# Splitting weights into a rounded and a rest part: casts by ScalarE and VectorE, or two DMAs of GpSimd

## The chip, the cores and the metric

The kernel runs on one core of a Trainium2 chip. A core has TensorE (PE: matrix products), VectorE (DVE), ScalarE (ACT) and GpSimd (POOL) for elementwise work, SyncE (SP) that here only issues DMAs, and 16 DMA engines between the chip's memory (HBM) and the core's own (SBUF). PE writes its results into eight banks of PSUM. Each engine works through a queue of its own, in order; an instruction whose inputs are not there yet holds up all that stand behind it in the same queue.

The metric is the time of the whole program on the device in microseconds (us), median of several runs.

## The reference, cut to what matters

Four layers of mixed kinds work on 1040 tokens (16 learned ones and 1024 of the input) with 1024 channels: attention over a sliding window, mLSTM, HGRN2, and attention again. Each layer normalizes its input, multiplies it by a large matrix, mixes over time, and multiplies by an output matrix:

```
for i in range(DEPTH):
    kind = i % N_MIXERS
    u = rmsnorm(h, norm_gain[i])
    if kind == 0:   y = attention_branch(u, a_w_in[j], ..., a_w_out[j], valid, pos)
    elif kind == 1: y = mlstm_branch(u, b_w_in[j], ..., b_w_out[j], valid)
    else:           y = hgrn2_branch(u, c_w_in[j], ..., c_w_out[j], valid)
    h = h + jnp.where(valid[None, :, None], y, 0.0)
```

All of it is float32. The change concerns the two products `u @ w_in` and `y @ w_out` alone, and in them only how the weights come into SBUF.

## The kernel before

**Products in two parts.** PE's faster format fp32r keeps fewer bits than float32. So the kernel splits each operand: `h` is the operand rounded to fp32r, `l` is what the rounding left (operand minus `h`, rounded in turn), and a product becomes three: h·h, h·l and l·h. The activations are split once into `uh` and `ul`; the weights are split tile by tile as they are loaded.

**Weight tiles.** A tile is 128 x 1024 numbers (512 KB), laid out by the host so that each of 128 partitions reads 4 KB in one run. There are 176 of them: 28 in each attention layer, 80 in the mLSTM layer, 40 in the HGRN2 layer. `proj` (line 242, matmuls on line 259) uses one tile for 128 output channels over three chunks of tokens (400, 384 and 256 columns), 72 matmuls per tile. `proj_v` (line 276, matmuls on lines 300 and 304) uses two tiles at a time, the two halves of the contraction, alternately for each block of 128 tokens. `proj_out` (line 320, matmuls on line 349) also holds two tiles, one for each half of the output channels.

**How a tile gets in.** `weights` (line 229) takes a buffer for `h` and one for `l` from two rings, tags `wh` and `wl`, of three buffers each. It works in two halves of 512 columns: SP loads the raw half into a ring of two buffers (`wr`, line 237); ScalarE rounds it into `h` (line 192); VectorE subtracts and writes `l` (line 193). Four pairs of tiles (`inrow=True`, one pair near the end of each layer) use buffers of the ring of rows, `r`, instead of `wh` and `wl`. One small matrix of the mLSTM layer goes through `gate_weights` (line 195), which takes a `wh` buffer for both of its parts.

**Order of the work.** The order of PE's instructions is written out by hand: `steps` is a list of (estimated PE time, function, preparation). The last loop of `hybrid_kernel` (line 1363) walks it and calls each tile's preparation, which is `weights`, as soon as the summed estimates between the step at hand and the tile's first use are below `LOOKAHEAD` (12000 ns). On the other engines a scheduler orders the instructions ahead of time from estimated durations; what was written earlier has priority. Buffers of a ring are handed out in turn, so a tile's `l` waits until PE has used the `l` three tiles earlier for the last time.

**What else is on POOL.** In the attention layers POOL writes the sink column of each score tile (line 630) and scales the exponentials by the reciprocal of their sum (line 638); PE's transposes of the result (line 650) wait for that. In the HGRN2 layer it copies small diagonal blocks (line 1169), in the mLSTM layer it sets a column of ones in each value tile (line 856). It issues no DMA.

Of the kernel before, what the change touches and what calls it, by code (L numbers as in the profile page):

```python
# [9 lines left out]
F32 = mybir.dt.float32  # L10
F32R = mybir.dt.float32r
AF = mybir.ActivationFunctionType
ALU = mybir.AluOpType
PSUM = bass.MemoryType.PSUM

P = 128
D = 1024
KT = D // P
# [13 lines left out]


B_COLS = 96
LOOKAHEAD = 12000.0
TAIL_LAG = 600.0
PRIO = 40
ROWS, TMPS, RAWS, YS = 8, 6, 2, 3
XS = 14
GAP, BURST = 200.0, 1300.0  # L40
KT_LAG, ATT_LAG = 900.0, 600.0
# [68 lines left out]
def hybrid_kernel(ctx: ExitStack, tc: tile.TileContext, ins, out, layers=(0, 1, 2, 3)):  # L110
    nc = tc.nc
    v, s, g, pe, sp = nc.vector, nc.scalar, nc.gpsimd, nc.tensor, nc.sync
# [3 lines left out]
    wpool = ctx.enter_context(tc.tile_pool(name="wpool", bufs=1))  # L116
# [7 lines left out]
    def nm(x):  # L124
        ctr[0] += 1
        return f"{x}{ctr[0]}"

    def row():
        return rpool.tile([P, T], F32, tag="r", name=nm("r"), bufs=ROWS)

    def rrow():
        return rpool.tile([P, T], F32R, tag="r", name=nm("r"), bufs=ROWS)
# [58 lines left out]
    def split(src, h, l):  # L191
        s.copy(h, src)  # L192
        v.tensor_tensor(l, src, h.bitcast(F32), op=ALU.subtract)  # L193

    def gate_weights(src):

        w = wpool.tile([P, 1024], F32R, tag="wh", name=nm("wh"), bufs=3).rearrange("p (k z c) -> p k z c", k=KT, z=2)
        raw = row()[:, :512]
        sp.dma_start(raw, src)
        raw = raw.rearrange("p (k c) -> p k c", k=KT)  # L200
        split(raw, w[:, :, 0], w[:, :, 1])
        return w

    def gate_rows_proj(src, evac):

        st = {}

        def pre():
            st["w"] = gate_weights(src)

        groups = []
        for n, (c0, cn) in enumerate(CHUNKS):
            grp = []
            for part in range(4):
                def fn(n=n, c0=c0, cn=cn, part=part):
                    if part == 0:
                        st[n] = psj()
                    for k in (2 * part, 2 * part + 1):
                        for i, b in enumerate((uh, ul)):
                            pe.matmul(st[n][:, :cn], st["w"][:, k].rearrange("p z c -> p (z c)"), b[:, k, c0 : c0 + cn],  # L220
                                      start=(k == 0 and i == 0), stop=(k == KT - 1 and i == 1))
                    if part == 3:
                        evac(st[n], n, c0, cn)

                grp.append([4 * cn * MM, fn, pre if (n == 0 and part == 0) else None])
            groups.append(grp)
        return groups

    def weights(src, kind, inrow=False):
        if inrow:  # L230
            h, l = (rrow()[:, :1024] for _ in range(2))
        else:
            h = wpool.tile([P, 1024], F32R, tag="wh", name=nm("wh"), bufs=3)
            l = wpool.tile([P, 1024], F32R, tag="wl", name=nm("wl"), bufs=3)
        for z in (slice(0, 512), slice(512, 1024)):
            raw = wpool.tile([P, 512], F32, tag="raw", name=nm("wr"), bufs=RAWS)
            sp.dma_start(raw, src[:, z])
            split(raw, h[:, z], l[:, z])
        k = dict(m=8, v=4, o=2)[kind]
        return h.rearrange("p (k c) -> p k c", k=k), l.rearrange("p (k c) -> p k c", k=k)  # L240

    def proj(src, evac, chunks=CHUNKS):
        st = {}

        def pre():
            st["w"] = weights(src, "m")

        groups = []
        for n, (c0, cn) in enumerate(chunks):
            grp = []  # L250
            for part in range(4):
                def fn(n=n, c0=c0, cn=cn, part=part):
                    if part == 0:
                        st[n] = psj()
                    h, l = st["w"]
                    acc = st[n]
                    for k in (2 * part, 2 * part + 1):
                        for i, (a, b) in enumerate(((h, uh), (h, ul), (l, uh))):
                            pe.matmul(acc[:, :cn], a[:, k, :], b[:, k, c0 : c0 + cn],  # L259
                                      start=(k == 0 and i == 0), stop=(k == KT - 1 and i == 2))  # L260
                    if part == 3:
                        evac(acc, n, c0, cn)

                grp.append([6 * cn * MM, fn, pre if (n == 0 and part == 0) else None])
            groups.append(grp)
        return groups
# [9 lines left out]
    def proj_v(src0, src1, evac):  # L276
        st = {}

        def pre0():
            st[0] = weights(src0, "v")  # L280

        def pre1():
            st[1] = weights(src1, "v")
# [1071 lines left out]
    ahead, k = 0.0, 0  # L1355
# [6 lines left out]
    k = 0  # L1362
    for n, (cost, fn, pre) in enumerate(steps):
        while k < len(steps) and (k <= n or ahead < LOOKAHEAD):
            if steps[k][2]:
# [119 lines left out]
```

## Time and profile before

| | us |
|---|---|
| three runs, median (lowest to highest) | 2641.04 (2640.87 to 2641.67) |
| the profiled execution | 2644.26 |
| its span, first to last instruction | 2642.5 |

The stretches of the span belong to: attention 0 to about 495, mLSTM to about 1590, HGRN2 to about 2190, attention again to the end. A row of the costliest groups names the line, the engine, the operation, the tile written and the tiles read, shape and count, then busy time in all and the mean of one, and at last the idle time of the engine just ahead of these instructions with what ended it. A matmul's duration in the trace is longer than the distance to the next one, since matmuls overlap in the pipeline; the distance is what it costs.

### The profile page before, as it was taken

How to read it: one execution, taken by the hardware profiler on the slowest of the kernel's cores; microseconds unless marked ns; L12 is line 12 of the kernel's file. 1: busy time of each engine (PE TensorE's matmuls, PEld its weight loads, DVE VectorE, ACT ScalarE, POOL GpSimd, SP SyncE). 2: the span in 40 equal slices, each digit the busy share in tenths (PEclk: the TensorE clock that was granted, in tenths of full speed). 3: DMA queues.
4: the chain of work that ended last, by engine and by line, in shares of the span. 5: the costliest groups of instructions: out<-in, count | busy, mean ns of one | idle time of the engine just before them, and what ended most of it. 6: DMA issues, size and time to landing. Idle time of an engine off the chain costs nothing.

```text
span 2642.5 us, 54003 instructions
## 1 busy us (share of the span) xinstructions
PE 2577.0 (98%) x20276; PEld 2476.4 (94%) x20276; DVE 1969.1 (75%) x5324; ACT 1688.6 (64%) x4339; POOL 247.2 (9%) x502
## 2 busy tenths in 40 slices
PE   7999999999999999999999999999999999999999
PEld 5899989999999999999999999999999998999999
DVE  6887797974747474746465688979887979887896
ACT  7777767555454545454545657878685857767773
POOL 2221221000000000000000000100000000321330
PEclk9999999999999999999999999999999999999999
DMA  4213111011111111111111101011110113212112
GB/s 129 67 50 91 47 44 43 26 61 56 41 57 41 57 41 57 41 57 41 53 45 49 49 26 50 30 38 34 34 42 30 38 50 91 59 42 83 55 37 80
DMA packets 82438, 136.10 MB, mean 52 GB/s; under 512 B 12016, under 2 KB 34928, under 8 KB 82176
## 3 DMA queue, kind: packets, MB, share of 16 engines
q1 hardware_dynamic: 82176, 132.65, 15.9%
q8 instruction: 160, 2.62, 0.4%
q14 instruction: 102, 0.84, 0.1%
HBM read 117.76 MB, written 4.26 MB: 46 GB/s over the span
## 4 chain that ended last, share of the span: by engine, by line
PE 74%; DVE 12%; ACT 8%; DMA 2%; issue 2%; SPq 1%; POOL 0%; DVEq 0%; ACTq 0%; POOLq 0%
PE pj L259 35%; PE pj L349 15%; PE pj L304 10%; PE po L669 1%; ACT Sm L635 1%; PE pt L650 1%; PE po L894 1%; PE pa L908 1%; PE po L896 1%; DVE wl L193 1%; DVE Sm L632 1%; SPq L523 1%; PE pm L1141 1%; PE pj L300 1%; ACT wh L192 1%
## 5 line engine op out<-in xcount | busy, mean ns | idle before, releaser
L259 PE MATMUL pj<-uh,wh 128*128 128x256 f32 (+2 forms) x2688 | 925.9, 344 | 9.6 <-ACT uh L192 9.4
L259 PE MATMUL pj<-ul,wh 128*128 128x256 f32 (+2 forms) x2688 | 867.1, 323 | 3.0 <-DVE ul L193 2.5
L259 PE MATMUL pj<-uh,wl 128*128 128x256 f32 (+2 forms) x2688 | 863.8, 321 | 0.0
L259 PEld LDWEIGHTS pj<-uh,wh 128*128 128x128 f32 x2688 | 509.4, 189 | 31.3 <-ACT uh L192 13.5
L259 PEld LDWEIGHTS pj<-ul,wh 128*128 128x128 f32 x2688 | 509.9, 190 | 16.3 <-DVE ul L193 6.7
L259 PEld LDWEIGHTS pj<-uh,wl 128*128 128x128 f32 x2688 | 509.3, 189 | 0.0
L192 ACT CAST wh<-wr 128x512 fp32r<-128x512 f32 x336 | 201.9, 615 | 99.1 <-PE pj L349 31.4
L193 DVE TENSOR_TENSOR wl<-wr,wh 128x512 fp32r<-128x512 f32 x336 | 232.3, 700 | 42.7 <-ACT wh L192 40.7
L349 PE MATMUL pj<-yh,wh 128*128 128x384 f32 (+2 forms) x768 | 253.1, 330 | 9.9 <-DVE x L352 6.7
L352 DVE TENSOR_TENSOR x<-x,pj 128x384 f32<-128x384 f32 (+2 forms) x480 | 234.6, 508 | 35.0 <-PE pj L349 33.6
L349 PE MATMUL pj<-yl,wh 128*128 128x384 f32 (+2 forms) x768 | 245.3, 319 | 0.3 <-DVE yl L193 0.3
L349 PE MATMUL pj<-yh,wl 128*128 128x384 f32 (+2 forms) x768 | 245.2, 319 | 0.0
L304 PE MATMUL pj<-wh,uh 128*128 128x256 f32 x768 | 231.7, 302 | 0.0
L304 PE MATMUL pj<-wh,ul 128*128 128x256 f32 x768 | 216.7, 282 | 0.0
L304 PE MATMUL pj<-wl,uh 128*128 128x256 f32 x768 | 216.5, 282 | 0.0
L635 ACT ACTIVATE Sm<-Sm,s 128x257 f32<-128x257 f32 (+2 forms) x272 | 130.7, 482 | 90.7 <-DVE s L632 89.4
L638 POOL TENSOR_TENSOR Sm<-Sm,s 128x512 f32<-128x512 f32 (+2 forms) x136 | 140.9, 1036 | 472.3 <-DVE s L637 451.6
L430 DVE SCALAR_TENSOR_TENSOR t<-pj,t 128x384 f32<-128x384 f32 (+2 forms) x192 | 98.7, 514 | 100.7 <-ACT t L429 99.7
L431 ACT ACTIVATE t<-t 128x384 f32<-128x384 f32 (+2 forms) x240 | 117.7, 490 | 82.2 <-DVE t L430 80.8
L349 PEld LDWEIGHTS pj<-yh,wh 128*128 128x128 f32 x768 | 144.1, 188 | 15.0 <-DVE x L352 8.9
L192 ACT CAST yh<-r 128x384 fp32r<-128x384 f32 (+2 forms) x120 | 57.1, 478 | 151.0 <-PE pj L349 134.3
L304 PEld LDWEIGHTS pj<-wh,uh 128*128 128x128 f32 x768 | 145.3, 189 | 2.1
(248 smaller groups left out, 5442.4 us busy)
## 6 DMA issues: line engine op xcount, KB each, us to landing
wr<-in_b_win SPq DMA_DIRECT2D x128, 256.0 KB, 2.8
wr<-in_a_win SPq DMA_DIRECT2D x80, 256.0 KB, 2.8
wr<-in_c_win SPq DMA_DIRECT2D x64, 256.0 KB, 2.8
wr<-in_a_wout SPq DMA_DIRECT2D x32, 256.0 KB, 2.8
wr<-in_b_wout SPq DMA_DIRECT2D x32, 256.0 KB, 2.8
t<-t SPq DMA_DIRECT2D x104, 48.0 KB, 1.9
cs<-in_rope SPq DMA_DIRECT2D x11, 400.0 KB, 3.3
cs<-in_rope SPq DMA_DIRECT2D x11, 384.0 KB, 3.6
```

Of the source, the lines that this page charges most:

```text
L192: s.copy(h, src)
L193: v.tensor_tensor(l, src, h.bitcast(F32), op=ALU.subtract)
L259: pe.matmul(acc[:, :cn], a[:, k, :], b[:, k, c0 : c0 + cn], start=(k == 0 and i == 0), stop=(k == KT - 1 and i == 2))
L300: pe.matmul(acc[:48, :256], um[0][:, k, :], m[:, kk, :], start=(k == 0 and m is wh), stop=(k == KT - 1 and m is wl))
L304: pe.matmul(acc[:cn, :256], a[:, k, c0 : c0 + cn], m[:, kk, :], start=(k == 0 and i == 0), stop=(k == KT - 1 and i == 2))
L349: pe.matmul(acc[:, :cn], a[:, k, mc], b, start=(k == 0 and i == 0), stop=(k == 1 and i == 2))
L352: v.tensor_tensor(x[:, m, c0 : c0 + cn], x[:, m, c0 : c0 + cn], acc[:, :cn], op=ALU.add)
L430: v.scalar_tensor_tensor(a[:, :cn], z, 0.0, a[:, :cn], op0=ALU.min, op1=ALU.subtract)
L431: s.activation(a[:, :cn], a[:, :cn], AF.Exp)
L523: sp.dma_start(rot[32 * q : 32 * q + 32], dst[32 * o : 32 * o + 32])
L635: s.activation(Sm[:nq, u, : nk + 1], Sm[:nq, u, : nk + 1], AF.Exp, scale=-1.0, bias=st[:nq, u : u + 1], accum_out=den[:nq, u : u + 1])
L638: g.tensor_tensor(Sm[:nq, :, :nk], Sm[:nq, :, :nk], den[:nq].rearrange("p (u c) -> p u c", c=1).to_broadcast([nq, 2, nk]), op=ALU.mult)
```

## The change

Weights no longer pass through raw buffers. A DMA issued by GpSimd loads the whole tile straight into the fp32r buffer `h` and rounds on the way. ScalarE writes `-h` into `l`. A second DMA of GpSimd reads the same tile from HBM again and adds it to `l`, which then holds tile minus `h`. The ring `raw` is gone and `wh` has a fourth buffer (its size is that of the two raw buffers); `wl` keeps three. `LOOKAHEAD` goes from 12000 to 16000. `gate_weights` keeps its old way, save for the ring's new length.

```
-LOOKAHEAD = 12000.0
+LOOKAHEAD = 16000.0
...
-ROWS, TMPS, RAWS, YS = 8, 6, 2, 3
+ROWS, TMPS, YS = 8, 6, 3
...
-        w = wpool.tile([P, 1024], F32R, tag="wh", name=nm("wh"), bufs=3).rearrange("p (k z c) -> p k z c", k=KT, z=2)
+        w = wpool.tile([P, 1024], F32R, tag="wh", name=nm("wh"), bufs=4).rearrange("p (k z c) -> p k z c", k=KT, z=2)
...
-            h = wpool.tile([P, 1024], F32R, tag="wh", name=nm("wh"), bufs=3)
+            h = wpool.tile([P, 1024], F32R, tag="wh", name=nm("wh"), bufs=4)
             l = wpool.tile([P, 1024], F32R, tag="wl", name=nm("wl"), bufs=3)
-        for z in (slice(0, 512), slice(512, 1024)):
-            raw = wpool.tile([P, 512], F32, tag="raw", name=nm("wr"), bufs=RAWS)
-            sp.dma_start(raw, src[:, z])
-            split(raw, h[:, z], l[:, z])
+        g.dma_start(h, src)
+        s.activation(l, h.bitcast(F32), AF.Identity, scale=-1.0)
+        g.dma_start(l, src, accum_op=ALU.add)
```

## The prediction

> **What bounds the kernel now.** I read the page's busy times first, then the busy times by stretch, then what PE waited for.
>
> ```profile
> span 2642.5 us, 54003 instructions
> ## 1 busy us (share of the span) xinstructions
> PE 2577.0 (98%) x20276; PEld 2476.4 (94%) x20276; DVE 1969.1 (75%) x5324; ACT 1688.6 (64%) x4339; POOL 247.2 (9%) x502
> ```
>
> PE is idle for 2642.5 - 2577.0 = 65.5 us of the span. No change that takes work from other engines can gain more than about that. POOL, to which the change gives its DMAs, is nearly empty on average. Averages hide stages, so here are four stretches; the columns are PE, its weight loads, DVE, ACT and POOL, each with its count of instructions, then the granted clock, the DMA share and GB/s.
>
> ```profile
> 0.00:50.00 50.00, 32.95 (x118) 23.91 (x119) 32.84 (x62) 34.40 (x69) 9.79 (x16) 0.93 0.48 154
> ...
> 300.00:400.00 100.00, 94.44 (x637) 88.51 (x637) 87.18 (x245) 70.45 (x201) 29.33 (x47) 1.00 0.15 45
> ...
> 764.00:898.00 134.00, 134.00 (x887) 130.43 (x885) 79.87 (x202) 68.45 (x161) 0.88 (x9) 1.00 0.15 48
> ...
> 1740.00:1840.00 100.00, 99.97 (x1282) 94.98 (x1282) 91.71 (x297) 86.70 (x246) 10.50 (x28) 1.00 0.12 39
> ```
>
> The mLSTM layer, 764 to 898 for one of its eight heads, leaves PE no idle time: DVE and ACT have room there, and freeing them buys nothing. The start loses 17 us, and attention (300 to 400) loses 5.6 us in 100 while DVE is 87% busy and POOL 29%. What ended PE's longest waits:
>
> ```profile
> PE pa L534 <- ACT t L520: 9.6, 7, 2.3
> PE pj L259 <- ACT uh L192: 9.4, 8, 3.8
> PE pt L650 <- POOL Sm L638: 6.9, 6, 2.1
> PE pj L349 <- DVE x L352: 6.7, 6, 1.4
> ```
>
> Together 32.6 us, half of the idle time, none of it for weights. The splitting of weights is hidden today; removing it can help only by making DVE and ACT answer sooner.
>
> **What goes.**
>
> ```profile
> L192 ACT CAST wh<-wr 128x512 fp32r<-128x512 f32 x336 | 201.9, 615 | 99.1 <-PE pj L349 31.4 <-PE pj L259 21.0 <-DMA wr<-in_b_win 17.6
> L193 DVE TENSOR_TENSOR wl<-wr,wh 128x512 fp32r<-128x512 f32 x336 | 232.3, 700 | 42.7 <-ACT wh L192 40.7
> ```
>
> DVE loses 232 us, an eighth of its 1969, and the same two operations of the eight tiles in rows go besides. ACT loses 202 us.
>
> **What ACT gets back.** 176 instructions over 1024 columns.
>
> ```profile
> L192 ACT CAST uh<-t 128x256 fp32r<-128x256 f32 x32 | 12.5, 402 | 4.7 <-DVE t L413 4.6
> ```
>
> From 402 ns for 256 columns and 615 ns for 512 it is 0.83 ns a column, so about 1.04 us for 1024: 176 x 1.04 = 183 us. ACT's load stays nearly what it was. The relief is DVE's. Bounds for one: 0.6 us (the row for half a tile) to 1.23 us (two of them).
>
> **The new chain of a tile.** Before, once PE had given an `l` buffer free, one cast and one subtraction filled it. Now, from the same moment, ACT writes -h, POOL issues the adding DMA, and this must land. Its price:
>
> ```profile
> rb<-rowsd SPq DMA_DIRECT2D x8, 520.0 KB, 3.4
> wb<-rowsd SPq DMA_DIRECT2D x8, 520.0 KB, 4.2
> ```
> ```profile
> L237 SPq DMA_DIRECT2D wr<-in_b_win x128: 327/328/671, 441.6 to 1494.1; - x128
> ```
> ```profile
> L638 POOL TENSOR_TENSOR Sm<-Sm,s 128x512 f32<-128x512 f32 (+2 forms) x136 | 140.9, 1036 | 472.3 <-DVE s L637 451.6 <-PE pm L626 11.9 <-PE pt L650 5.1
> ```
>
> Plain transfers of this size land after 3.4 to 4.2 us. No DMA of the trace adds; it must read two sources, so it lies between 3.4 and twice 4.2 = 8.4 us, and I take 5, near the plain rows. POOL issues none either: between SP's 0.33 us and POOL's own usual 1.04 us (L638), I take 1.0, since POOL is the engine that will do it. With 0.5 us of queueing on ACT the chain is 0.5 + 1.04 + 1.0 + 5 = 7.5 us, and between 0.6 + 0.33 + 3.4 = 4.3 and, with 2 us of queueing, 2 + 1.23 + 1.04 + 8.4 = 12.7 us. The loading of `h` isn't in it: the fourth `wh` buffer lets it start one tile earlier. The Trainium skill (DMA: Bandwidth & Descriptors, "Anatomy of one DMA — SWDGE (gpsimd) path") gives 2.0 us plus the bytes by 436 GB/s for a GpSimd DMA, an estimate of 3.2 us here; by it the chain would be 5.7 us and the tight places below would cost 2 us rather than 7; no run so far shows one.
>
> **Where is that chain too long?** I counted the tiles in the order of the code and looked in the timeline for the last use of the `l` three tiles back and the first use of the new one. Usual places have room:
>
> ```profile
> 755.02 0.28 PE L304 MATMUL pj<-wl,uh 128*128 128x256 f32 x1
> ...
> 770.41 0.35 PE L259 MATMUL pj<-uh,wl 128*128 128x400 f32 x1
> ```
>
> That is 15.4 us, the scarcest kind in a steady mLSTM head, twice the chain. But where a pair of tiles meets a layer's beginning there is little room: the second `v` tile of the first mLSTM head, the second `v` tile of HGRN2, and the first `q` tile after it:
>
> ```profile
> 528.66 0.28 PE L259 MATMUL pj<-uh,wl 128*128 128x256 f32 x1
> ...
> 532.64 0.28 PE L300 MATMUL pj<-wl,um 128*48 128x256 f32 x1
> ```
> ```profile
> 1588.07 0.28 PE L349 MATMUL pj<-yh,wl 128*128 128x256 f32 x1
> ...
> 1594.23 0.28 PE L300 MATMUL pj<-wl,um 128*48 128x256 f32 x1
> ```
> ```profile
> 1619.37 0.28 PE L259 MATMUL pj<-uh,wl 128*128 128x256 f32 x1
> ...
> 1625.54 0.34 PE L259 MATMUL pj<-uh,wl 128*128 128x400 f32 x1
> ```
>
> From the end of the first matmul of each pair (0.28 us long) there are 3.7, 5.9 and 5.9 us. With 7.5 us PE stands still for 3.8 + 1.6 + 1.6 = **7 us**; with 4.3 us for 0.6; with 12.7 for 22.6. Nothing behind can win this back in the mLSTM layer, where PE is never idle. The longer `LOOKAHEAD` doesn't help here: the buffer, not the order, starts the chain, since I leave the ring `wl` at three.
>
> **POOL's queue.** The 352 DMAs take 1.0 us each of an engine that is 9% busy. What stands behind them matters: L638, for which PE's transposes wait, often with no reserve:
>
> ```profile
> 284.58 0.66 POOL L638 TENSOR_TENSOR Sm<-Sm,s 128x288 f32<-128x288 f32 x1 [3.23 <-DVE s L637]
> ```
> ```profile
> 285.35 0.20 PE L650 MATMUL pt<-ident,Sm 16*16 16x16 f32 x2
> ```
>
> Here PE starts 0.11 us after POOL ends (285.24). The two attention layers have 28 tiles, so 56 DMAs, each in some 480 us: POOL is issuing for 12% of the time. Of 136 L638, 12% lose half an issue: 136 x 0.12 x 0.5 = 8 us; only 6 of them ended a wait of PE, others have reserve, so I count a third, 2.7 us. Besides, a DMA that waits at the head (the adding one for ACT, the loading one for a free `wh`) holds L638 and L630 up. ACT stood 99.1 us ahead of its 336 casts, 0.3 us each; the same before 112 DMAs is 34 us of 960, 3.5% of the time, for which I add 2 us. Together **5 us**, between 0 and 43 (a rival below). In HGRN2 and mLSTM POOL's copies and memsets have fewer followers; I count nothing, and if L1169 lost its cover it would show as a wait of L1222.
>
> **The start.** The first chunk of x lands at 6.5 us and the norm follows:
>
> ```profile
> 2.12 4.42 DMA x<-in_xT
> ```
>
> Today the weights are issued behind it on SP. From POOL's queue three whole tiles (1.5 MB) set out beside 1.6 MB of x. At worst the 4.4 us double; I take half, 2.2 us, and against it that the second and third tile no longer queue for raw buffers: **+2 us**, from -3 to +5.
>
> **The relief.** DVE's load is an eighth lighter, so its part and what queues behind it of the 32.6 us shrinks; L520 and the casts of `uh` are ACT's, which stays as full. I take a fifth: **-6 us**, bounds 0 and a half (-16). One rule of the Trainium skill bears on it (SBUF — State Buffer, "Who interferes with whom"): a DVE instruction with two SBUF inputs, such as L193, shuts out a GpSimd instruction that reads SBUF, so L638 would get faster too; by this rule it would be a few us more gain, and no run shows it apart. The same section speaks against the change: VectorE's two-port modes keep GpSimd from writing descriptors, which would stretch the chain by the length of one such DVE instruction.
>
> **Sum.** 7 + 5 + 2 - 6 = +8 us, against the profiled execution's 2644.26 (span and 1.8 us around it), which is 3.2 above the median of the runs. I carry the 8 us over to the median: 2641.0 + 8 = **2649.0 us**. A difference under 0.2% (5.3 us) can't be told from none.
>
> **The rivals.**
> 1. *Slightly slower, the forecast*, 2644 to 2665: chance 0.33.
> 2. *Faster by DVE's relief*: the chain is 4.3 us, so the tight places cost 0.6, POOL's issues cost 1 and the start nothing, and half of the 32.6 us goes: 0.6 + 1 - 16 = -14, 2627 us. It decides once an adding DMA lands within about 4 us and attention's waits for DVE are worth more than POOL's delays. For it: DVE at 87 to 92% in two kinds of layer. Against it: PE's idle time sits mostly behind ACT and the start. Chance 0.25.
> 3. *Hidden anyway*, 2641, within 0.2%: costs and relief cancel, as PE at 98% suggests. Chance 0.20.
> 4. *POOL's head blocks attention*: the adding DMA waits up to 4 us in POOL's queue for ACT. 28 such waits and 4 us in 480 are 23%, the loading DMAs' waits as much again: 136 x 0.47 x 2 us, a third of it, 43 us instead of 5: 2687 us. Against it: the order is planned ahead, and of the 472 us that POOL idled ahead of L638, 452 were ended by DVE's own result. Chance 0.14.
> 5. *The adding DMA is slow*: past 15 us the chain passes the usual mLSTM place too. At 18 us eight heads lose 18 - 15.1 = 2.9 us each, 23 us, and the three tight places 38: 2641 + 23 + 38 + 5 + 2 - 6 = 2703 us. Chance 0.08.
>
> That the DMA doesn't round, so that `l` would come out zero, would leave the time as it is; no chance of its own. Most chance lies on slower: rivals 1, 4 and 5 without the forecast's edge under 2646 give 0.53; same 0.22; faster 0.25. The range leaves out a tenth on each side: 2625 to 2690.
>
> **What would show it.** Right: the mLSTM heads still 134 us apart; new waits of L300 and L259 for a DMA into `wl` at about 532, 1594 and 1625, some 7 us together; an adding DMA that lands about 5 us after its issue; more than 6.9 us of waits of L650 for L638; DVE about 1725 us busy, ACT about 1660. Wrong: waits for `wl` inside mLSTM heads (rival 5), POOL standing for us at DMA issues ahead of L638 (rival 4), or PE's waits for L352 and L520 gone and none new (rival 2).

## The result, and the profile after

| | before | after |
|---|---|---|
| median of four runs, us | 2640.95 | 2675.88 |
| lowest to highest | 2640.47 to 2641.67 | 2673.09 to 2682.88 |
| the profiled execution, us | 2644.26 | 2682.88 |

The ratio is 1.0136, with a 95% interval of 1.0116 to 1.0156: 35 us slower, where 8 us were forecast. The profiled execution after is the slowest of its four runs, 7 us above their median; that much of the differences below is its own. In the file after, lines beyond 234 have numbers lower by one (L299 is L300 of before, L637 is L638); the loading DMA is L235, the negation L236, the adding DMA L237. In the experiments they shift again by a few lines; the names of the tiles stay.

The first part of the page after, busy times, and the third, DMA queues with packets, MB and their share of the 16 engines' time:

```profile
span 2681.1 us, 53343 instructions
...
PE 2592.4 (97%) x20276; PEld 2493.6 (93%) x20276; DVE 1773.3 (66%) x4972; ACT 1675.5 (62%) x4163; POOL 489.0 (18%) x854
...
q0 software_dynamic: 50688, 184.57, 30.5%
```

DVE is relieved by 196 us and ACT by 13. PE nevertheless has more idle time, 2681.1 - 2592.4 = 88.7 us instead of 65.5, and is also 15 us longer busy with the same matmuls, but most of that is this execution's own: look, an experiment below with the same median, was profiled at 2670.89 us, and there PE is busy for 2579.5 us. POOL's queue of DMAs, q0, which did not exist before, alone takes 30.5% of the DMA engines' time. What ended PE's longest waits after:

```profile
PE pj L258 <- ACT uh L192: 12.9, 8, 4.7
PE pa L390 <- DVE t L382: 12.9, 5, 5.1
PE pt L649 <- POOL Sm L637: 11.6, 3, 4.9
...
PE pt L581 <- ACT t L574: 7.8, 4, 4.7
PE pj L299 <- DMA wl<-in_b_win: 3.6, 1, 3.6
...
PE pj L299 <- DMA wl<-in_c_win: 2.8, 1, 2.8
...
PE pj L258 <- DMA wl<-in_c_win: 1.1, 1, 1.1
```

The three waits for `wl` are there, 7.5 us together. But the larger growth stands at old places: the start (`uh`, `t` of L382) and attention (L649, L581). PE's matmuls come in the same order in both kernels, so the start of the k-th can be set against the start of the k-th. Difference to before in us, worked out from the records of the profiled executions:

```
time in before           60    520    560   1580   1660   2180   end
after                   11.1   25.5   30.1   30.3   35.3   31.9   38.5
first tiles old way     -2.0    6.4   10.0   10.0   15.2   12.1   15.1
no adding DMA            3.1   -2.0   -3.7   -2.8   -3.7   -7.7   -9.6
none in attention        2.9   -3.0   -0.3   -0.3    4.1   -0.8   -1.4
none in tight places     9.6   20.5   17.4   17.4   16.4   13.0   16.4
copies by SP             3.2   11.5   10.9   10.9   11.1   11.2    9.8
copies by POOL          27.5  126.6  124.3  124.3  124.4  124.6  123.8
```

The row "after" is the place to begin: 11 us at the start, 14 in the first attention layer (60 to 520), 5 at each of the two layer beginnings (520 to 560 and 1580 to 1660), nothing in the mLSTM heads, 3 won in HGRN2, 7 lost in the second attention layer. The other rows belong to experiments below.

**The start.** The chain of waits of after, in order of time, and two rows of ACT's timeline:

```profile
3.07 9.56 DMA x<-in_xT
...
12.65 12.07 DMA x<-in_xT
...
24.73 3.56 DMA x<-in_xT
```
```profile
27.26 0.42 ACT L378 ACTIVATE r<-x 128x256 f32<-128x256 f32 x1 [6.43 <-DMA x<-in_xT]
27.58 0.51 ACT L192 CAST uh<-t 128x400 fp32r<-128x400 f32 x1
```

For 25 of its first 28 us the kernel waits for `x` alone. ACT's queue is in order: the square of the third chunk waits 6.43 us for its data, and the cast of `uh`, for which PE waits, stands behind it. So a chunk that nobody needs yet delays the first product.

**Attention.** One stall of 4.91 us, from several engines' timelines after:

```profile
89.88 0.89 POOL L237 DMA_DIRECT2D wl<-in_a_win  x1 [3.08 <-ACT t L518]
...
92.02 0.59 SPq L522 DMA_DIRECT2D t<-t  x1
...
93.47 0.88 POOL L237 DMA_DIRECT2D wl<-in_a_win  x1 [2.14 <-ACT t L365]
98.55 0.42 DVE L538 TENSOR_TENSOR t<-t,cs 128x256 f32<-128x256 f32 x1 [3.09 <-DMA t<-t]
...
101.85 0.21 PE L649 MATMUL pt<-ident,Sm 16*16 16x16 f32 x2 [4.91 <-POOL Sm L637]
```

The row of PE names POOL, but POOL was idle. Read backwards: L637 waited for DVE's L636; DVE's queue stood for 3.09 us at L538, which needs a rotation `t<-t` of 32 KB. SP issued its last piece at 92.02 and this landed at 98.36, 6.3 us later. Ahead of it were an adding DMA and a loading one, which was issued at 90.43 and landed at 98.20, and behind it another adding DMA. The landings of the tiles `t` in before:

```profile
DMA to landing us min/median/max: 1.8/1.9/4.1
```

There none took over 4.1 us. The name behind a wait is the last link; the cause stood three links earlier.

**A tight place.** PE's timeline after, and the granted clock (third number from the end) in the stretches around it:

```profile
559.50 0.28 PE L299 MATMUL pj<-wh,um 128*48 128x256 f32 x1
563.34 0.45 PE L299 MATMUL pj<-wl,um 128*48 128x256 f32 x1 [3.56 <-DMA wl<-in_b_win]
563.59 0.41 PE L299 MATMUL pj<-wh,um 128*48 128x256 f32 x1
```
```profile
563.30:566.30 3.00, 2.96 (x14) 2.86 (x15) 1.58 (x1) 1.19 (x2) 0.00 (x0) 0.50 0.18 66
566.30:569.30 3.00, 3.00 (x17) 3.00 (x16) 2.42 (x8) 0.54 (x2) 1.17 (x8) 0.53 0.32 34
```

The wait is 3.56 us, as forecast (3.8). Behind it PE is busy, but for 6 us at half its clock, 0.50 and 0.53: a matmul of the same form takes 0.41 us instead of 0.28. That loses time which no row of waits counts; it is part of the 15 us that PE is longer busy. Behind the second wait, 2.78 us, the granted clock was 0.55 for 3 us; behind the third, 1.15 us, it stayed at 1.00. It isn't the same in every execution: in look's profile the second wait was 2.54 us, and the clock behind it stayed at 1.00. The Trainium skill has this rule (TensorE: Matmul & The Clock Gate, "What's actually happening"): an idle window of about 3.4 us halves the clock until about as long a busy one has passed. The trace agrees in the factor; the slow stretch here is nearer 6 us, and a wait of 2.78 us was enough.

### The profile page after: what moved, and what is told of

Read it like the earlier page. It is cut to its first block, busy times and chain, and to the rows that moved or that the text cites. A ratio compares the mean times of both kernels' runs of the same rounds, so it can differ in the third digit from the quotient of the medians.

```text
span 2681.1 us, 53343 instructions
## 1 busy us (share of the span) xinstructions
PE 2592.4 (97%) x20276; PEld 2493.6 (93%) x20276; DVE 1773.3 (66%) x4972; ACT 1675.5 (62%) x4163; POOL 489.0 (18%) x854
## 3 DMA queue, kind: packets, MB, share of 16 engines
q0 software_dynamic: 50688, 184.57, 30.5%
## 4 chain that ended last, share of the span: by engine, by line
PE 79%; DVE 7%; ACT 5%; DMA 4%; issue 4%; SPq 1%; POOL 0%; DVEq 0%; ACTq 0%; POOLq 0%
PE pj L258 39%; PE pj L348 15%; PE pj L303 9%; PE po L668 2%; PE pt L649 2%; DMA cs<-in_rope 1%; PE po L893 1%; DMA t<-t 1%; PE pa L907 1%; PE pm L1140 1%; PE po L895 1%; ACT Sm L634 1%; DMA x<-in_xT 1%; PE pm L624 1%; PE pm L625 1%
## 5 line engine op out<-in xcount | busy, mean ns | idle before, releaser
L258 PE MATMUL pj<-uh,wh 128*128 128x256 f32 (+2 forms) x2688 | 930.1, 346 | 13.0 <-ACT uh L192 12.9
L236 ACT ACTIVATE wl<-wh 128x1024 fp32r<-128x1024 f32 x168 | 177.4, 1056 | 112.9 <-DMA wh<-in_b_win 32.3
L637 POOL TENSOR_TENSOR Sm<-Sm,s 128x512 f32<-128x512 f32 (+2 forms) x136 | 137.0, 1007 | 299.4 <-DVE s L636 293.9
L348 PEld LDWEIGHTS pj<-yl,wh 128*128 128x128 f32 x768 | 145.8, 190 | 3.5 <-DVE yl L193 3.2
```

The lines of the kernel that those rows point to most:

```text
L236: s.activation(l, h.bitcast(F32), AF.Identity, scale=-1.0)
L258: pe.matmul(acc[:, :cn], a[:, k, :], b[:, k, c0 : c0 + cn], start=(k == 0 and i == 0), stop=(k == KT - 1 and i == 2))
L348: pe.matmul(acc[:, :cn], a[:, k, mc], b, start=(k == 0 and i == 0), stop=(k == 1 and i == 2))
L637: g.tensor_tensor(Sm[:nq, :, :nk], Sm[:nq, :, :nk], den[:nq].rearrange("p (u c) -> p u c", c=1).to_broadcast([nq, 2, nk]), op=ALU.mult)
```

## The experiments

The theory that the traces suggested, A: the DMAs of 512 KB from POOL's queue run on the same 16 engines as SP's transfers and delay those that are on the path (`x` at the start, rotations and rope tables in attention), besides the tight places. Rivals: B, POOL's queue holds its attention work up; C, ACT's 1.06-us negations delay the evacuations; D, the longer `LOOKAHEAD` alone. Two further beliefs are tried at the end.

**Without the adding DMA (noadd).** Leaves the tile out of `l`.

```
         s.activation(l, h.bitcast(F32), AF.Identity, scale=-1.0)
-        g.dma_start(l, src, accum_op=ALU.add)
```

> The new path without its adding DMA: l holds only the negated h (the tile itself is not added to it). Half of POOL's traffic, 0.88 of the 1.43 us that POOL spends on issuing for a tile, and the landing in the chain of a tile go; ScalarE's 1.06-us negations stay. Theory A (POOL's bulk transfers delay SP's transfers of x, of the rope tables and of the rotations): the tight places' 9 us go, about half of the start's 12 us and about half of the 22 us of both attention layers: 2676 - 9 - 6 - 11 = 2650 us, and the transfers of x land in about 6 us instead of 8.2. Theory B (POOL's queue holds its own attention work up): the start stays, two thirds of attention's 22 us go: 2676 - 9 - 14 = 2653 us, x still at 8.2 us. Theory C (ScalarE's negations delay the evacuations): only the tight places go, 2667 us. Theory D (the longer LOOKAHEAD): 2667 us.

Measured: 2634.32 us, ratio to before 0.9975 (0.9966 to 0.9985). That is 42 us below after, more than any theory gave, and it falls at the start, in attention and in the tight places (row "no adding DMA" of the table above). The negations are all still there: C falls. The order is that of `LOOKAHEAD` 16000: D has little left.

**LOOKAHEAD alone (look).**

```
-LOOKAHEAD = 16000.0
+LOOKAHEAD = 12000.0
```

> Only LOOKAHEAD back from 16000 to 12000. Theories A, B and C: within 4 us of 2676, either way, since the ring's buffers and not the order start a tile's chain. Theory D (written earlier, the negations have priority over the evacuations in ScalarE's planned order, and POOL's issues over its attention work): at least 10 us less, 2666 or below.

Measured: 2676.57 us, ratio 1.0132 (1.0117 to 1.0148), after's own. D falls.

**The first four tiles by the old way (start).**

```
+        if tiles[0] <= 4:
+            raw = row()
+            for z in (slice(0, 512), slice(512, 1024)):
+                sp.dma_start(raw[:, z], src[:, z])
+                split(raw[:, z], h[:, z], l[:, z])
+        else:
             g.dma_start(h, src)
```

> The first four tiles come by the old way (SP loads raw halves into a row, ScalarE casts, VectorE subtracts), all others by the new one. Theory A: the start's delay against the kernel before, 12 to 14 us at PE's first hundred matmuls, goes: 2676 - 12 = 2664 us, x lands in 4 to 5 us again. If the start's delay has been swallowed later anyway (PE would wait in the first attention layer for the same things): no change, 2676 us. My prediction's own term of 2 us for the start would give 2674 us.

Measured: 2659.98 us, ratio 1.0079 (1.0064 to 1.0094), 16 us less. The start is as fast as before (-2.0 us at 60), the gain stays to the end, and `x` lands as it did before the change. The rows are SP's issues of `x` with the median from issue to landing, first after, then this kernel:

```profile
x<-in_xT SPq DMA_DIRECT2D x8, 200.0 KB, 8.3
```
```profile
x<-in_xT SPq DMA_DIRECT2D x8, 200.0 KB, 4.0
```

**Four buffers for l, three for h (swap).**

```
-            h = wpool.tile(..., tag="wh", ..., bufs=4)
-            l = wpool.tile(..., tag="wl", ..., bufs=3)
+            h = wpool.tile(..., tag="wh", ..., bufs=3)
+            l = wpool.tile(..., tag="wl", ..., bufs=4)
```

> The ring wl has four buffers and wh three, so a tile's chain of negation and adding DMA can start one tile earlier, while the loading of h starts one tile later. If the three tight places cost what the trace shows there (4.5, 3.0 and 1.9 us, with a slower clock for some us behind each): their waits of L300 and L258 for the DMA into wl go, 2676 - 10 = 2666 us. Rival: the wait moves to wh (an h lands 3.6 us after its issue, and it too is now released a tile later, so neg and adding DMA follow it): 2676 us or more.

Measured: 2717.28 us, ratio 1.0293 (1.0275 to 1.0312), 41 us slower than after: the rival, and stronger than I gave it. PE's waits in this kernel:

```profile
PE pj L258 <- DMA wl<-in_a_win: 10.3, 4, 3.9
PE pj L299 <- DMA wl<-in_b_win: 8.1, 2, 5.6
```

They are still waits for `wl`. That fits the rival: when `h` is loaded a tile later, load, negation and adding DMA stand in a row, and a spare `l` is of no use. By the times, the new way needs its fourth `wh` buffer more than it would a fourth `wl`.

**POOL kept busy without traffic (busy).** `l` holds the negated `h`.

```
-        g.dma_start(l, src, accum_op=ALU.add)
+        g.tensor_copy(l[:, :384], l[:, :384].bitcast(F32))
```

> The new path without its adding DMA, but with POOL kept as long: at the place of each adding DMA, POOL copies 384 columns of l in place (about 0.9 us, after ScalarE's negation, as the DMA's issue was); l holds the negated h alone. Without the adding DMA the time was 2634.3 us. Theory A (the adding DMA's traffic and landing cost the time): 2634 plus at most 4 us. Theory B (POOL's queue, by the issues and their waits for ScalarE at its head, holds its attention work up): the 20 us that attention lost come back, 2650 us or more; in the trace, L649's waits for L637 are as long as with the adding DMA.

Measured: 2631.09 us, ratio 0.9957 (0.9940 to 0.9973). The group of these copies on POOL, and PE's wait for POOL, in this kernel:

```profile
L237 POOL CAST wl<-wl 128x384 fp32r<-128x384 f32 x168 | 93.7, 558 | 212.7 <-ACT wl L236 187.1 <-issue 19.4 <-ACT s L897 4.2
```
```profile
PE pt L649 <- POOL Sm L637: 6.5, 3, 2.3
```

A copy took 0.56 us, not the 0.9 I wanted, so POOL was held for two thirds as long as by the adding DMA's 0.88 us. But the waits at the head of its queue for ACT's negations were there (187.1 us), and L649 waited no longer than in before. By B some 13 of 20 us should have come back; none did. B falls.

**A second DMA that does not add (plain).** `l` holds the rounded tile.

```
-        g.dma_start(l, src, accum_op=ALU.add)
+        g.dma_start(l, src)
```

> Both DMAs of a tile, in the same queue with the same waits, but the second one rounds the tile over the negated h instead of adding to it; l then holds the rounded tile. If adding is what is dear (it reads SBUF too): the second DMA lands like the first, after 3.6 us instead of 5.3 to 6.3, the tight places' 9 us shrink to 2, and of the 9 us at the start and 20 us of attention that the adding DMA brought, most goes: 2650 us or less. If another 512 KB of traffic as such is dear: only the tight places' share and some of the rest goes, 2660 to 2668 us. Theory B: as that, 2665 to 2669 us, since POOL's issues and waits stay.

Measured: 2651.28 us, ratio 1.0038 (1.0023 to 1.0053). So the 42 us split: 17 for a second transfer of each tile, 25 for its adding. Landing and share of the DMA engines say why; after, then noadd, then this kernel:

```profile
wl<-in_b_win POOLq DMA_DIRECT2D x64, 512.0 KB, 6.3
...
wl<-in_c_win POOLq DMA_DIRECT2D x32, 512.0 KB, 5.3
```
```profile
q0 software_dynamic: 25344, 92.29, 11.4%
```
```profile
q0 software_dynamic: 50688, 184.57, 23.1%
...
wl<-in_b_win POOLq DMA_DIRECT2D x64, 512.0 KB, 4.7
```

The loading DMAs take 11.4% of the engines' time. A plain second set adds 11.7, an adding one 30.5 - 11.4 = 19.1: adding costs 1.6 times a plain transfer of the same bytes.

**The same traffic beside the old way (traf_sp, traf_pool).** One copy of each tile from HBM to HBM that nothing reads, issued by SP or by POOL.

```
+        sp.dma_start(dram.tile([P, 1024], F32, tag="dump", ..., bufs=8), src)
```

> The kernel before, with one more transfer for each tile: SP copies the tile's 512 KB from HBM to a scratch place in HBM that nothing reads. Theory A: traffic alone delays the small transfers on which attention and the start depend: 2641 + 10 us or more, with t<-t of 32 KB and x landing later than 1.9 and 4.0 us. Theory B: no POOL instruction is added, within 4 us of 2641.

> The kernel before, with the same extra copy of each tile from HBM to a scratch place in HBM, but issued by POOL: its transfers stand in another queue than SP's. Theory A (bulk transfers beside SP's delay those that attention and the start need): 2641 plus 10 to 20 us, with DVE's waits for the rope tables and rotations above the 20.9 us of before. If the 14 us of the same copies from SP came from SP's own queue being longer: within 4 us of 2641.

Measured: 2656.08 us from SP, ratio 1.0054 (1.0039 to 1.0069); 2762.07 from POOL, ratio 1.0459 (1.0443 to 1.0476). The dose was not what I meant: in both kernels all 176 copies were issued within the first 460 us. But it was much the same in both. The stretch from 60 to 460 us, with DMA share and GB/s at the end, the landings of the 32 KB rotations in it, and DVE's wait for rotations, ahead of its operations on tile `cs`, with the copies from POOL:

```profile
60.00:460.00 400.00, 305.56 (x1856) 284.38 (x1855) 243.33 (x650) 227.83 (x613) 137.18 (x255) 0.88 0.73 249
```
```profile
t<-t SPq DMA_DIRECT2D x28, 32.0 KB, 4.7
```
```profile
  DMA t<-t: 79.8, 16
```

The first two of these with the copies from SP:

```profile
60.00:460.00 400.00, 380.81 (x2514) 360.05 (x2513) 327.38 (x889) 293.73 (x809) 91.85 (x144) 0.98 0.80 270
```
```profile
t<-t SPq DMA_DIRECT2D x36, 32.0 KB, 2.2
```

With the copies in POOL's queue the first attention layer loses about 100 us (last row of the table of differences), its rotations of 32 KB land in 4.7 us instead of 1.9, DVE waits 79.8 us for rotations instead of 3.8, and the DMA engines are on average only 73% busy. From 460 us on the copies have ended and nothing more is lost: the later layers, the second attention layer among them, run as before. SP's queue holds nothing new here. PE's waits for POOL's scaling grew too, from 6.9 to 17.2 us, but far less than the waits for rotations. So bulk copies from POOL do delay SP's small transfers.

With the same copies in SP's own queue the traffic was as heavy, 270 GB/s and 80%, and it cost 14 us in all, 8 of them in this layer. The first chunk of `x` landed after 4.3 us (4.4 in before, 18.6 with the copies from POOL), and DVE's wait for rotations was 4.7 us. The slowest rotation of the stretch whose landing the trace gives took 4.5 us here, 6.4 in after, 23.7 with the copies from POOL. So the amount of traffic alone doesn't explain the delay, against what I expected from theory A; here the bulk did its harm from another queue than the small transfers'. SP issues its copies a few at a time between its rotations; whether this is the reason, no run shows. The Trainium skill says (DMA: Bandwidth & Descriptors, "Issuing engines are not separate DMA queues") that DMAs of all issuers run on the same 16 engines and interleave. The delays of SP's transfers by POOL's agree with that, but at like traffic the issuer made a difference of 106 us here.

**Where the adding DMAs are dear (add_off_att, add_off_tight).** Without them in the two attention layers, and without them for three tiles only.

```
-        g.dma_start(l, src, accum_op=ALU.add)
+        if not src.tensor.name.startswith("in_a"):
+            g.dma_start(l, src, accum_op=ALU.add)
```
```
+        seen.append((src.tensor.name, kind))
+        if seen.count(seen[-1]) != 2 or seen[-1] not in (("in_b_win", "v"), ("in_c_win", "v"), ("in_c_win", "m")):
             g.dma_start(l, src, accum_op=ALU.add)
```

> The changed kernel, but tiles of the two attention layers get no adding DMA (their l holds the negated h alone); mLSTM and HGRN2 keep it. Without any adding DMA the time fell by 42 us. Theory A, by where the matmuls of the changed kernel lost against those without adding: some 9 us at the start, 14 and 6 us in the two attention layers, the rest in the tight places: 2676 - 29 = 2647 us, between 2642 and 2652. If the adding DMAs are as dear in the other layers (by their traffic or by ScalarE's and POOL's queues): 56 of 176 tiles are a third, 2676 - 42 x 0.32 = 2663 us.

> The changed kernel, but three tiles get no adding DMA: the second v tile of the first mLSTM head, the second v tile of HGRN2 and the first q tile behind it. If these are the tight places: PE's three waits for wl (3.6, 2.8 and 1.1 us) go and with them the slower clock behind them, 2676 - 10 = 2666 us, the gain in those places alone. Rival: the next tile of the ring takes the wait over, since its chain starts from the same release: 2671 us or more. My prediction's term for the three was 7 us.

Measured: 2644.35 us, ratio 1.0013 (1.0005 to 1.0022), and 2663.02 us, ratio 1.0084 (1.0070 to 1.0098). So 56 attention tiles, the start's among them, cost 31.5 us, three tight tiles 12.9, and the 117 others next to nothing: 31.5 + 12.9 = 44.4 against the 41.6 of all. By the intervals of the ratios each of the two is uncertain by about 6 us. Two stretches of after, the first in attention, the second one mLSTM head, with GB/s at the end:

```profile
60.00:500.00 440.00, 415.94 (x2680) 396.13 (x2679) 321.36 (x885) 309.24 (x817) 129.89 (x201) 0.96 0.35 83
...
764.00:898.00 134.00, 134.00 (x886) 130.43 (x885) 68.92 (x183) 67.48 (x150) 14.90 (x29) 1.00 0.37 87
```

The traffic is as heavy in the head, 87 GB/s against 83, and PE, which is never idle there, loses nothing to it: no transfer stands on the path. What DVE's rope operations (tile `cs`) waited for, in before, after, add_off_att:

```profile
  DMA cs<-in_rope: 11.9, 8
  DMA r<-r: 5.2, 1
  DMA t<-t: 3.8, 6
```
```profile
  DMA t<-t: 22.3, 16
  DMA cs<-in_rope: 21.1, 7
  DMA r<-r: 9.8, 2
```
```profile
  DMA t<-t: 11.3, 15
  DMA cs<-in_rope: 9.7, 6
  DMA r<-r: 7.8, 2
```

From 20.9 us to 53.2 and back to 28.8.

**Is there a better version? (sub_half, sub_pool).** noadd and busy show that what the change relieves, DVE above all, is worth 7 to 11 us where no adding DMA spoils it. So: the old way, with one or both subtractions of a tile on POOL, which has room.

```
-                split(raw, h[:, z], l[:, z])
+                s.copy(h[:, z], raw)
+                g.tensor_tensor(l[:, z], raw, h[:, z].bitcast(F32), op=ALU.subtract)
```

(in sub_half `(g if z.start else v)` for `g`)

> The kernel before, with the subtraction of the second half of each tile (128x512) on POOL instead of DVE: no transfer is added, DVE loses half of its 246 us, POOL gains about 176 x 1.13 = 199 us. If what helps is DVE's relief, and POOL's queue is no hindrance (as the copies on POOL showed, 2631 us): 2641 - 4 = 2637 us, between 2633 and 2641. If two engines that read SBUF at once slow each other: 2641 or more.

> As the kernel before, with both subtractions of every tile on POOL: DVE loses 246 us, POOL gains about 352 x 1.13 = 398 us and is then 24% busy. By DVE's relief alone: 2641 - 8 = 2633 us. If 2.3 us of POOL for a tile are too many ahead of its attention work (POOL's queue, in the form in which it could still hold): the attention layers lose more than the rest gains, 2645 us or more.

Measured: 2674.33 us, ratio 1.0130 (1.0113 to 1.0147), and 2702.53 us, ratio 1.0228 (1.0213 to 1.0243). A clear miss. Two groups of DVE in before, then the page's busy times and the same groups in sub_pool:

```profile
L352 DVE TENSOR_TENSOR x<-x,pj 128x384 f32<-128x384 f32 (+2 forms) x480 | 234.6, 508 | 35.0 <-PE pj L349 33.6
...
L439 DVE TENSOR_TENSOR r<-r,t 128x384 f32<-128x384 f32 (+2 forms) x120 | 61.5, 513 | 1.4
```
```profile
PE 2595.6 (96%) x20276; PEld 2487.5 (92%) x20276; DVE 1906.0 (71%) x4972; ACT 1686.2 (63%) x4339; POOL 699.8 (26%) x854
...
L353 DVE TENSOR_TENSOR x<-x,pj 128x384 f32<-128x384 f32 (+2 forms) x480 | 235.3, 509 | 43.6 <-PE pj L350 42.2
...
L440 DVE TENSOR_TENSOR r<-r,t 128x384 f32<-128x384 f32 (+2 forms) x120 | 83.5, 696 | 1.9
```

After runs the same 4972 instructions on DVE in 1773 us, sub_pool in 1906. `r<-r,t`, with both inputs in SBUF, goes from 513 to 696 ns; `x<-x,pj`, with one in PSUM, stays at 509. The Trainium skill's rule (SBUF — State Buffer, "Who interferes with whom") says that a DVE instruction with two inputs in SBUF contends with a GpSimd instruction that reads SBUF, and that one with at most one, outside the two-port modes, doesn't; these two rows agree with it. No kernel here that does the whole computation is faster than the one before.

## Why the prediction was right or wrong

The sign and the range were right; the likeliest value, 8 us, was 27 too low. That the range held was luck: 2675.88 us lies above the 2644 to 2665 that the forecast gave its own mechanism, and the range reached further up only because of rivals (the fourth at 2687 us, the fifth at 2703) whose mechanisms the runs don't show. Two groups of after that its steps need, the negation and the scaling on POOL, with the mean of one as the second number behind the bar:

```profile
L236 ACT ACTIVATE wl<-wh 128x1024 fp32r<-128x1024 f32 x168 | 177.4, 1056 | 112.9 <-DMA wh<-in_b_win 32.3 <-PE pj L258 31.0 <-PE pj L348 29.8
```
```profile
L637 POOL TENSOR_TENSOR Sm<-Sm,s 128x512 f32<-128x512 f32 (+2 forms) x136 | 137.0, 1007 | 299.4 <-DVE s L636 293.9 <-PE pt L649 5.1
```

By its steps:

- **Tight places, +7.** The right three, and the waits sum to 7.5 us. The chain was near: negation 1.06 us, issue 0.88, landing 5.3 to 6.3 for the 5 I took; the 3.2 us worked out there for any GpSimd DMA were too few for an adding one, and the loading ones took 3.8 (tiles of `in_b_win`). But the three tiles cost 12.9 us (add_off_tight), give or take 6. The sum didn't contain the slow clock behind the first two waits. From 6 us at about half and 6 us at 0.55 to 0.89 I estimate that it lost 4.6 us in the profiled execution, 12.1 with the waits.
- **POOL's queue, +5.** Wrong. This step priced attention's loss by POOL's issues and the waits at its head. With POOL held for two thirds as long by copies instead of adding DMAs, that loss was gone (busy). What attention lost by, and the prediction had no term for, is SP's small transfers landing late: of the 31.5 us of add_off_att some 23 lie in the two attention layers, since adding brought about 8 at the start (11.1 - 3.1 at 60 us).
- **The start, +2.** The mechanism, POOL's tiles beside `x`, was named; the size was 11 us instead of 2 (the row after at 60 us), and taking the first four tiles back won 16. The step halved "the 4.4 us double" and looked at the first chunk only. In fact the transfers of the first chunk did double (8.3 us against 4.0 in start), the later chunks came late too (8.9 and 5.6 us for 4.0 and 3.6 in before), and ACT's queue passed the third chunk's lateness on to the first product. The first chunk isn't what mattered most: in noadd it took 8.5 us as well, the later ones 6.1 and 3.2, and the start lost 3.1 us.
- **The relief, -6.** About right: 7 us gained in noadd, 11 in busy, mostly in HGRN2 and attention. The rule on ports that I weighed there shows weakly: L637 takes 1007 ns where L638 took 1036. The stretched issues that I weighed against the change don't show: an adding DMA's took 0.85 to 1.07 us.
- **The signs.** mLSTM heads unchanged: right, 30.1 us behind at 560, 30.3 at 1580. More waits of PE for L638: they came, 11.6 us for 6.9, and would have seemed to prove the step on POOL, yet POOL wasn't their cause; the sign was badly chosen. DVE 1773 us and ACT 1676 busy, not 1725 and 1660.
- **Rivals.** The second needed a landing within about 4 us and attention's relief above POOL's delays; without the adding DMA the kernel did become faster, by 7 us. The third, no difference, lies outside the interval. The fifth, a slow adding DMA, needed a chain past 15 us and didn't occur. The fourth, POOL's head, gave a time 11 us too high by a mechanism that the runs exclude.

The failing step has one form: an added transfer was priced by its own landing and by the engine that issues it, and at one place by what it does to others. With measured sizes the sum is 13 (tight) + 31 (start and attention) - 7 (relief and the rest, noadd) = 37, against 35.

What stays open: whether the small transfers wait for their turn on the DMA engines or for memory behind them, why the same copies cost 14 us from SP's queue and 120 from POOL's, and how the relief would fare without the added traffic in a kernel that does the whole computation.

## What to carry to other kernels

A bulk DMA that moves to another engine's queue is priced by the small transfers beside it: look for those on the path (here rotations of 32 KB and the first loads), and ask what the in-order queues behind them hold. Three waits of PE that summed to 7.5 us cost about 12.9, so add the slow clock behind the longer ones. An engine that looks nearly idle may share a port with the one that it is to relieve.

## What the hardware showed that I had not expected

- After a wait of 3.56 us PE's granted clock was 0.50 and 0.53 for 6 us, after one of 2.78 us 0.55 for 3 us, after one of 1.15 us it stayed at 1.00.
- An adding DMA of 512 KB landed in 6.3 us where a second plain one took 4.7 (tiles of `in_b_win`), and it took 1.6 times the engine time.
- A transfer of 32 KB that landed in 1.9 us in before took 4.7 in the median beside copies from POOL's queue (249 GB/s in all, the engines 73% busy), but 2.2 beside the same copies from its own queue (270 GB/s, 80%).
- DVE's two-input instructions became up to 36% longer (513 to 696 ns) while POOL subtracted.
